# Windowed attention blocks of a hybrid encoder: negated maximum, sink exponential and row scaling moved from VectorE to ScalarE

## The chip, the cores and the metric

The kernel runs on one core of one Trainium2 chip. A core has five engines that run their own queues in order: PE (TensorE, matrix products and transposes; PEld are its weight loads), DVE (VectorE), ACT (ScalarE), POOL (GpSimd) and SP (SyncE, which here only issues DMAs). They wait for one another through semaphores. The metric is the device time of one execution in microseconds (us), the median of three runs.

## The reference, cut to what matters

The program is a two-layer encoder over 512 tokens and 1024 channels. In each layer three token mixers read one projection: windowed attention (6 query heads, 2 key/value heads), a gated DeltaNet in chunks of 64 tokens, and an RWKV-7 scan; then come an output projection and a gated MLP. The change lies in the softmax of the attention:

```python
m = jnp.maximum(jnp.max(s, -1, keepdims=True), sk)      # sk: the head's sink logit
p = jnp.exp(s - m)
p = p / (jnp.sum(p, -1, keepdims=True) + jnp.exp(sk - m))
o = jnp.einsum('bnhgqk,bnkhd->bnqhgd', p.astype(v.dtype), vw)
```

A block of 128 queries sees its own 128 keys and those of the neighbouring blocks: 384 keys in the two middle blocks, 256 in the two outer ones.

## The kernel before, in words

Everything is float32. Long products (`product`, lines 332 to 334) are done as three passes over split operands, for which ACT and POOL prepare the weights (L321, L322).

`attn_head` does one pair of query heads (g = 0, 1) as a generator of four blocks. There are three such pairs, so 12 blocks per layer and 24 in the program. A block goes through these steps, with their lines before the change:

- L886, PE: two score products into PSUM.
- L887, DVE: adds the mask, writes the scores to SBUF (`cv`) and gives the row maximum with the sink in it (`mx`); a second small instruction reads the maximum out.
- L891, DVE: sink minus maximum (`es`). L892, DVE: negated maximum (`nmx`). L893, ACT: exponential of `es`. All are 128x2.
- L896, ACT, once for each g: exponential of the scores with `nmx` as bias; a small instruction then reads the row sums (`den`).
- L897 and L898, DVE: `den` plus `es`, and its reciprocal.
- L900, DVE, once for each g: the rows of `cv` times the reciprocal.
- L903, PE: two or three 128x128 transposes. L905, ACT: their copy out of PSUM. L907, PE: the products with the values. At the end of a head pair L909 copies the result.

The blocks have no stage of their own. In `layer` they are interleaved with the DeltaNet:

```python
for i in range(31):
    next(both_ways)
    if i % 6 == 5:
        next(att, None)
```

`both_ways` is `invert_both`: a forward substitution on 32x32 blocks, 30 steps, each of one multiply (L432) and one add (L433) on DVE, in which every instruction needs the one before it. So five attention blocks are issued in the inversion. Four stream transposes on DVE (L440, L441) end it, and `finish_inverse` follows: small PE products (L455, L461) with ACT copies (L457, L465, L469) between them. Then comes `dn_scan`: 8 steps, each a chain of PE products (L806, L817, L794) and DVE instructions (L813, L822, L796, L802), with output products (L832, L833) beside it; in each of its steps one more block is issued until the 12 are done. Long products of the gate projection (L974 to L977 read them) and of the output projection fill PE in between. The order on each engine is not the order of the text: a scheduler places each instruction by its own costs when the program is built, so that a change of one instruction's engine moves others too.

Of the kernel before, what the change touches and what calls it, by code (L numbers as in the profile page):

```python
# [10 lines left out]
AF = mybir.ActivationFunctionType  # L11
# [104 lines left out]
def trunk(tc, t, out):  # L116
    nc = tc.nc
    V, S, G, PE = nc.vector, nc.scalar, nc.gpsimd, nc.tensor
    mult, add, sub, mx, mn = ALU.mult, ALU.add, ALU.subtract, ALU.max, ALU.min
# [15 lines left out]
    def ps(stream, shape=(P, T)):  # L135
        return psp.tile(list(shape), F32, tag="ps" + stream, bufs=PS_BUFS[stream], name=nm("ps"))
# [4 lines left out]
    def t2(stream, *free, dt=F32):  # L141
        return bp.tile([P, *(free or (T,))], dt, tag="t" + stream, bufs=T_BUFS[stream], name=nm("t" + stream))

    def cv(*free, dt=F32):
        return bp.tile([P, *(free or (T,))], dt, tag="cv", bufs=8, name=nm("cv"))
# [13 lines left out]
    def tiny(*free, tag="tiny"):  # L159
        if len(free) > 1:  # L160
            lo = W + DEPTH * NPAR + 2 * T + 48 * small_at.setdefault(tag, len(small_at))
            names = " ".join("abc"[: len(free)])
            return fixed[:, lo : lo + math.prod(free)].rearrange(f"p ({names}) -> p {names}", **dict(zip("abc", free)))
        return bp.tile([P, *free], F32, tag=tag, bufs=1 if len(free) > 1 else 3, name=nm(tag))


    W = _CONST.shape[1]
# [6 lines left out]
    def C(name):  # L174
        a, n = CONSTS[name]
        return cst[:, a : a + n]
# [697 lines left out]
    def attn_head(l, tq, q, k, vt, dst):  # L874
        po = ps("r")
        for nb in range(4):
            k0, k1 = max(0, nb - 1), min(3, nb + 1)
            nk = k1 - k0 + 1
            W = P * nk
            m0 = P * (k0 - nb + 1)  # L880
            scs = [cv(), cv()]
            mxt = tiny(2, tag="mx")
            for g in range(2):
                hs = slice(64 * g, 64 * g + 64)
                pss = ps("r")
                PE.matmul(pss[:, :W], q[hs, P * nb : P * nb + P], k[hs, P * k0 : P * k0 + W], start=True, stop=True)  # L886
                V.tensor_tensor_reduce(scs[g][:, :W], pss[:, :W], C("attm")[:, m0 : m0 + W], 1.0, sinkb[l][:, tq + 3 * g : tq + 3 * g + 1], add, mx, mxt[:, g : g + 1])  # L887
            sk = sinkb[l][:, tq : 6 : 3]
            nmx = tiny(2, tag="nmx")
            es = tiny(2, tag="es")  # L890
            V.tensor_tensor(es, sk, mxt, sub)  # L891
            V.tensor_scalar(nmx, mxt, -1.0, None, mult)  # L892
            S.activation(es, es, AF.Exp)  # L893
            den = tiny(2, tag="den")
            for g in range(2):
                S.activation(scs[g][:, :W], scs[g][:, :W], AF.Exp, bias=nmx[:, g : g + 1], accum_out=den[:, g : g + 1])  # L896
            V.tensor_tensor(den, den, es, add)  # L897
            V.reciprocal(den, den)  # L898
            for g in range(2):
                V.tensor_scalar(scs[g][:, :W], scs[g][:, :W], den[:, g : g + 1], None, mult)  # L900
                pp = ps("r")
                for j in range(nk):
                    PE.transpose(pp[:, P * j : P * j + P], scs[g][:, P * j : P * j + P], ident)  # L903
                pt = t2("r")
                S.activation(pt[:, :W], pp[:, :W], AF.Copy)  # L905
                for j in range(nk):
                    PE.matmul(po[64 * g : 64 * g + 64, P * nb : P * nb + P], vt[:, k0 + j, 64 * g : 64 * g + 64], pt[:, P * j : P * j + P], start=j == 0, stop=j == nk - 1)  # L907
            yield
        S.activation(dst, po, AF.Copy)  # L909


    def layer(l, norm, xd, last):
# [81 lines left out]
        def attention():  # L994
            for tq in range(3):
                yield from attn_head(l, tq, qs[tq], k, vt, yt[tq])
# [155 lines left out]
```

## Time and profile before

| | |
|---|---|
| runs | 1709.49, 1710.0, 1717.93 us, median 1710.0 |
| the profiled execution | 1722.8 us, of which the span 1721.0 us |
| busy share of the span | PE 90%, weight loads 70%, DVE 57%, ACT 46%, POOL 37% |
| mean granted TensorE clock | 0.931 of full speed |

The trace is of the profiled execution, so its stretches add up to the span of 1721.0 us and not to the median. The share of an engine is an average over stages with different limits. The stretch from 315 to about 450 us is the inversion, its finish and the DeltaNet scan of layer 0, and the same stretch of layer 1 begins at about 1158 us. In these the attention blocks lie.

### The profile page before, as it was taken

The numbers are of one execution on the slowest core, as the hardware profiler recorded it, in microseconds if no ns is written. First come the engines' busy times: TensorE is split into PE (matmuls) and PEld (weight loads), VectorE is DVE, ScalarE is ACT, GpSimd is POOL, SyncE is SP. The second block draws the span as 40 slices with busy tenths as digits, with TensorE's granted clock in tenths as the row PEclk, the third lists the DMA queues.
The fourth block names the chain that finished last, engine by engine and source line by source line (L and its number), as shares of the span: only waits on it lengthen the run. The fifth ranks groups of instructions, "written<-read, shape, count | busy, mean of one in ns | idle before, by whom it ended". The sixth has DMA issues, their size and how long they took to land. (4 is left out here: it accounts for less than half of the span.)

```text
span 1721.0 us, 29049 instructions
## 1 busy us (share of the span) xinstructions
PE 1544.2 (90%) x11500; PEld 1208.7 (70%) x11500; DVE 973.5 (57%) x1595; ACT 792.0 (46%) x1493; POOL 638.7 (37%) x510
## 2 busy tenths in 40 slices
PE   7988889569999999999998887983899999999997
PEld 4676666347778888888876666652677788888885
DVE  6578946875535557731136797579563555555001
ACT  5547453355444444433336654351734544444321
POOL 4321323101265554445552112420104555555553
PEclk9989979669999999999999998995799999999998
DMA  6221211100143333333442012220003333333331
GB/s 185 73 57 38 56 38 44 37 2 20 36 122 96 98 98 95 96 104 114 119 101 68 25 45 50 55 70 1 4 19 93 102 95 97 98 99 114 101 101 65
DMA packets 230536, 126.07 MB, mean 73 GB/s; under 512 B 23656, under 2 KB 221416, under 8 KB 230400
## 3 DMA queue, kind: packets, MB, share of 16 engines
q1 hardware_dynamic: 228624, 121.02, 25.0%
q10 hardware_dynamic: 1776, 3.20, 0.6%
q8 instruction: 90, 1.47, 0.3%
q14 instruction: 46, 0.38, 0.1%
HBM read 117.84 MB, written 6.34 MB: 72 GB/s over the span
## 5 line engine op out<-in xcount | busy, mean ns | idle before, releaser
L322 POOL TENSOR_TENSOR wl<-wr,wh 128x512 fp32r<-128x512 f32 (+1 forms) x408 | 553.6, 1363 | 753.2 <-ACT wh L321 664.2
L332 PE MATMUL ps<-hh,wh 128*128 128x512 f32 x1248 | 505.2, 405 | 22.1 <-ACT wh L321 19.6
L333 PE MATMUL ps<-hl,wh 128*128 128x512 f32 x1248 | 504.5, 404 | 0.0
L334 PE MATMUL ps<-hh,wl 128*128 128x512 f32 x1248 | 500.9, 401 | 0.4 <-POOL wl L322 0.4
L321 ACT ACTIVATE wh<-wr 128x512 fp32r<-128x512 f32 (+1 forms) x408 | 246.2, 615 | 330.8 <-PE ps L333 262.4
L332 PEld LDWEIGHTS ps<-hh,wh 128*128 128x128 f32 x1248 | 237.8, 191 | 80.9 <-ACT wh L321 20.4
L333 PEld LDWEIGHTS ps<-hl,wh 128*128 128x128 f32 x1248 | 238.0, 191 | 56.8 <-issue 4.2
L334 PEld LDWEIGHTS ps<-hh,wl 128*128 128x128 f32 x1248 | 237.5, 190 | 56.8 <-issue 3.9
L1104 DVE TENSOR_TENSOR p<-ps,p 128x512 f32<-128x512 f32 x16 | 11.1, 692 | 196.6 <-PE ps L334 196.6
L332 PE MATMUL ps<-p,wh 128*128 128x512 f32 x256 | 99.6, 389 | 0.0
L333 PE MATMUL ps<-p,wh 128*128 128x512 f32 x256 | 99.6, 389 | 0.0
L334 PE MATMUL ps<-p,wl 128*128 128x512 f32 x256 | 99.6, 389 | 0.0
L903 PE MATMUL ps<-fixed,cv 128*128 128x128 f32 x120 | 24.9, 340 | 62.4 <-DVE cv L900 62.0
L1081 DVE TENSOR_TENSOR tr<-ps,rb 128x512 f32<-128x512 f32 x44 | 30.4, 691 | 80.9 <-PE ps L334 80.8
L292 POOL TENSOR_TENSOR tr<-tr,tr 128x512 f32<-128x512 f32 x32 | 42.6, 1332 | 70.4 <-ACT tr L285 59.9
L903 PEld LDWEIGHTS ps<-fixed,cv 128*128 128x128 f32 x120 | 16.0, 168 | 72.5 <-issue 44.8
L1084 DVE SCALAR_TENSOR_TENSOR td<-tr,fixed,td 128x511 f32<-128x511 f32 x44 | 42.8, 972 | 37.7 <-ACT td L1083 37.7
L285 ACT ACTIVATE tr<-p 128x512 f32<-128x512 f32 x36 | 22.6, 628 | 85.9 <-DVE p L1104 64.4
L791 POOL TENSOR_TENSOR sm<-sm,fixed 128x384 f32<-128x384 f32 x12 | 10.8, 896 | 121.5 <-DVE sm L820 64.5
L333 PEld LDWEIGHTS ps<-p,wh 128*128 128x128 f32 x256 | 48.1, 188 | 10.1
L332 PEld LDWEIGHTS ps<-p,wh 128*128 128x128 f32 x256 | 48.1, 188 | 10.1
L1084 DVE SCALAR_TENSOR_TENSOR tr<-td,fixed,tr 128x511 f32<-128x511 f32 x44 | 33.9, 771 | 37.5 <-ACT tr L1083 37.5
(294 smaller groups left out, 2559.7 us busy)
## 6 DMA issues: line engine op xcount, KB each, us to landing
wr<-ffn_w_up SPq DMA_DIRECT2D x176, 256.0 KB, 2.8
wr<-w_in SPq DMA_DIRECT2D x88, 256.0 KB, 2.9
wr<-ffn_w_down SPq DMA_DIRECT2D x80, 256.0 KB, 2.9
wr<-w_in SPq DMA_DIRECT2D x24, 128.0 KB, 2.4
p<-scr ACTq DMA_DIRECT2D x12, 256.0 KB, 3.5
wr<-w_out SPq DMA_DIRECT2D x32, 96.0 KB, 2.6
wr<-w_out SPq DMA_DIRECT2D x16, 192.0 KB, 2.9
p<-xt SPq DMA_DIRECT2D x8, 256.0 KB, 5.0
```

The costliest lines, as they stand in the source:

```text
L285: S.activation(sq, xk, AF.Square)
L292: G.tensor_tensor(acc, self.acc, sq, add)
L321: S.activation(hi[:, :n, :], raw[:, :n, :], AF.Copy)
L322: G.tensor_tensor(lo[:, :n, :], raw[:, :n, :], hi[:, :n, :].bitcast(F32), sub)
L332: PE.matmul(o, wh, xh, start=k == 0, stop=False)
L333: PE.matmul(o, wh, xl, start=False, stop=False)
L334: PE.matmul(o, wl, xh, start=False, stop=k == n - 1)
L791: G.tensor_tensor(gs, state, flat(gl, step), mult)
L903: PE.transpose(pp[:, P * j : P * j + P], scs[g][:, P * j : P * j + P], ident)
L1081: V.tensor_tensor(u, o, nf.rb, mult)
L1084: V.scalar_tensor_tensor(a[:, 1:], u[:, :-1], w(0), a[:, 1:], mult, add)
L1104: V.tensor_tensor(x1[j], o, x1[j], add)
```

## The change

Three pieces of a block go from DVE to ACT. The negated maximum becomes an ACT copy with scale -1. The subtraction for the sink and its exponential over both heads become one ACT exponential for each head, with the negated maximum as bias, each placed behind that head's score exponential. The scaling of the rows by the reciprocal becomes an ACT copy with a column as scale.

```diff
             nmx = tiny(2, tag="nmx")
             es = tiny(2, tag="es")
-            V.tensor_tensor(es, sk, mxt, sub)
-            V.tensor_scalar(nmx, mxt, -1.0, None, mult)
-            S.activation(es, es, AF.Exp)
+            S.activation(nmx, mxt, AF.Copy, scale=-1.0)
             den = tiny(2, tag="den")
             for g in range(2):
                 S.activation(scs[g][:, :W], scs[g][:, :W], AF.Exp, bias=nmx[:, g : g + 1], accum_out=den[:, g : g + 1])
+                S.activation(es[:, g : g + 1], sk[:, g : g + 1], AF.Exp, bias=nmx[:, g : g + 1])
             V.tensor_tensor(den, den, es, add)
             V.reciprocal(den, den)
             for g in range(2):
-                V.tensor_scalar(scs[g][:, :W], scs[g][:, :W], den[:, g : g + 1], None, mult)
+                S.activation(scs[g][:, :W], scs[g][:, :W], AF.Copy, scale=den[:, g : g + 1])
```

In the changed kernel the lines of a block are L891 (negated maximum), L894 (score exponential), L895 (sink exponential), L896 and L897 (sum and reciprocal), L899 (scaling), L902 (transposes), L904 (their copy), L906 (products with the values) and L908.

The scheduler moves other instructions with it. On DVE, in the inversion of layer 0 at the second block (`cv_2948` and `cv_2949` are its scores, `pair_sq` the matrix under inversion), the difference reads:

```order
 L432 TENSOR_TENSOR cv_2887<-pair_sq 128x396
+L433 TENSOR_TENSOR pair_sq<-pair_sq,cv_2887 128x2x22x9
 L887 ISA cv_2948,mx_2950<-ps_2951,fixed 128x384
 L887 ISA mx_2950 128x1
-L433 TENSOR_TENSOR pair_sq<-pair_sq,cv_2887 128x2x22x9
+L432 TENSOR_TENSOR cv_2887<-pair_sq 128x420
 L887 ISA cv_2949,mx_2950<-ps_2954,fixed 128x384
 L887 ISA mx_2950 128x1
-L432 TENSOR_TENSOR cv_2887<-pair_sq 128x420
-L891 TENSOR_TENSOR es_2958<-fixed,mx_2950 128x2
-L892 TENSOR_SCALAR nmx_2957<-mx_2950 128x2
 L433 TENSOR_TENSOR pair_sq<-pair_sq,cv_2887 128x2x21x10
```

One more inversion instruction now stands ahead of each of the block's two maxima.

On ACT, in the finish of the inversion of layer 0 with the fifth block in it (`cv_3099` and `cv_3100`; `p_1880` and `p_2690` are matrices into which the inverse is written):

```order
+L469 ACTIVATE p_1880<-p_3137 32x8x32
+L894 ACTIVATE cv_3099,den_3111<-cv_3099,nmx_3108 128x256
+L895 ACTIVATE es_3109<-fixed,nmx_3108 128x1
+L894 ACTIVATE cv_3100,den_3111<-cv_3100,nmx_3108 128x256
+L895 ACTIVATE es_3109<-fixed,nmx_3108 128x1
+L469 ACTIVATE p_2690<-p_3137 32x8x32
 L457 ACTIVATE td_3146<-ps_3145 32x512 x2
+L469 ACTIVATE p_2690<-p_3137 32x8x32 x2
+L899 ACTIVATE cv_3099<-cv_3099,den_3111 128x256
+L899 ACTIVATE cv_3100<-cv_3100,den_3111 128x256
 L469 ACTIVATE p_2690<-p_3137 32x8x32
+L904 ACTIVATE tr_3122<-ps_3119 128x256
```

The two scalings now stand in ACT's queue among the copies of the inverse.

On PE, in a step of the scan of layer 0 with a wide block, it stood before in this order (`ps_4031` and `ps_4041` take the transposes, `ps_4114` is the scan's new state, `tr_4035` and `tr_4045` the copied transposes):

```order
L903 MATMUL ps_4031<-fixed,cv_4011 128x128 x3
L903 MATMUL ps_4041<-fixed,cv_4012 128x128 x3
L833 MATMUL ps_4070<-p_2780,sm_3992 64x64
L832 MATMUL ps_4070<-p_2767,sm_3893 64x64
L833 MATMUL ps_4070<-p_2780,sm_3992 64x64
L817 MATMUL ps_4114<-sm_4111,p_1921 64x64
L907 MATMUL ps_3896<-tr_4035,at_2291 64x128 x3
L907 MATMUL ps_3896<-tr_4045,at_2291 64x128 x3
L817 MATMUL ps_4114<-sm_4111,p_1921 64x64 x3
L817 MATMUL ps_4114<-sm_4111,p_2731 64x64 x4
L817 MATMUL ps_4114<-sm_4111,p_2820 64x64 x4
```

and with the change in this one:

```order
L833 MATMUL ps_4070<-p_2780,sm_3992 64x64
L333 MATMUL ps_4436<-hl_4402,wh_4441 128x512
L817 MATMUL ps_4114<-sm_4111,p_1921 64x64
L902 MATMUL ps_4031<-fixed,cv_4011 128x128 x3
L817 MATMUL ps_4114<-sm_4111,p_1921 64x64 x2
L902 MATMUL ps_4041<-fixed,cv_4012 128x128 x3
L817 MATMUL ps_4114<-sm_4111,p_1921 64x64
L817 MATMUL ps_4114<-sm_4111,p_2731 64x64 x4
L817 MATMUL ps_4114<-sm_4111,p_2820 64x64
L906 MATMUL ps_3896<-tr_4035,at_2291 64x128 x3
L906 MATMUL ps_3896<-tr_4045,at_2291 64x128 x3
L817 MATMUL ps_4114<-sm_4111,p_2820 64x64 x3
```

The transposes now stand among the state products instead of ahead of them, and a product of the output projection (`ps_4436`) has come between.

## Rows read from the trace of the kernel before

**Rows 1.** The page: busy time and share, and the chain that ended last.

```profile
PE 1544.2 (90%) x11500; PEld 1208.7 (70%) x11500; DVE 973.5 (57%) x1595; ACT 792.0 (46%) x1493; POOL 638.7 (37%) x510
PE 31%; DVE 6%; issue 2%; ACT 1%; POOL 1%; DMA 0%; POOLq 0%; DVEq 0%; SPq 0%; ACTq 0%
```

**Rows 2.** Busy time by stretches: engines (instructions), granted clock (PEclk), DMA.

```profile
315.00:364.00 49.00, 19.15 (x74) 11.74 (x76) 45.36 (x114) 10.01 (x33) 0.21 (x1) 0.57 0.02 6
364.00:376.00 12.00, 7.24 (x169) 5.93 (x170) 10.14 (x16) 9.12 (x24) 0.00 (x0) 0.50 0.00 1
376.00:383.00 7.00, 6.12 (x138) 4.02 (x138) 1.40 (x6) 6.52 (x16) 0.00 (x0) 0.95 0.01 4
383.00:393.00 10.00, 10.00 (x150) 7.38 (x145) 0.56 (x1) 7.58 (x19) 0.00 (x0) 0.53 0.01 2
400.00:450.00 50.00, 46.95 (x860) 37.57 (x859) 32.15 (x107) 22.64 (x66) 7.15 (x7) 1.00 0.07 18
1350.00:1700.00 350.00, 350.00 (x1539) 289.64 (x1539) 140.72 (x183) 145.53 (x231) 183.12 (x139) 1.00 0.33 95
```

**Rows 3.** Single lines: duration in ns min/median/max, first and last start, shapes.

```profile
L900 DVE TENSOR_SCALAR cv<-cv,den x48: 332/394/420, 328.1 to 1290.2; 128x256 f32<-128x256 f32 x24, 128x384 f32<-128x384 f32 x24
L896 ACT ACTIVATE cv<-cv,nmx x48: 491/548/604, 326.0 to 1288.9; 128x256 f32<-128x256 f32 x24, 128x384 f32<-128x384 f32 x24
L893 ACT ACTIVATE es<-es x24: 189/203/205, 325.9 to 1288.3; 128x2 f32<-128x2 f32 x24
L475 ACT ACTIVATE p<-tr,fixed x16: 723/724/725, 29.3 to 910.2; 128x512 f32<-128x512 f32 x16
```

**Rows 4.** DVE in time, inversion, layer 0: start, us, instruction, idle and its releaser.

```profile
336.23 0.59 DVE L432 TENSOR_TENSOR cv<-pair_sq 128x420 f32<-128x420 f32 x1
336.88 0.59 DVE L433 TENSOR_TENSOR pair_sq<-pair_sq,cv 128x420 f32<-128x420 f32 x1
339.47 0.63 DVE L433 TENSOR_TENSOR pair_sq<-pair_sq,cv 128x456 f32<-128x456 f32 x1
340.68 0.64 DVE L432 TENSOR_TENSOR cv<-pair_sq 128x468 f32<-128x468 f32 x1
341.35 0.65 DVE L433 TENSOR_TENSOR pair_sq<-pair_sq,cv 128x468 f32<-128x468 f32 x1
...
360.41 0.43 DVE L433 TENSOR_TENSOR pair_sq<-pair_sq,cv 128x260 f32<-128x260 f32 x1
361.28 0.38 DVE L432 TENSOR_TENSOR cv<-pair_sq 128x216 f32<-128x216 f32 x1
```

**Rows 5.** DVE in time, the row maxima of the second and third block.

```profile
333.06 0.62 DVE L887 CUSTOM_DVE_ANT_0 cv<-ps,fixed 128x384 f32<-128x384 f32 x1 [0.29 <-PE ps L886]
335.69 0.62 DVE L887 CUSTOM_DVE_ANT_0 cv<-ps,fixed 128x384 f32<-128x384 f32 x1 [1.51 <-PE ps L886]
...
345.83 0.62 DVE L887 CUSTOM_DVE_ANT_0 cv<-ps,fixed 128x384 f32<-128x384 f32 x1 [0.37 <-PE ps L886]
```

**Rows 6.** ACT in time, end of the finish of the inversion, layer 0.

```profile
388.67 0.78 ACT L465 ACTIVATE p<-ps 32x256 f32<-32x256 f32 x2 [1.44 <-PE ps L461]
```

**Rows 7.** PE in time, one step of the scan with a wide block.

```profile
436.09 0.92 PE L794 MATMUL ps<-sm,cv 64*64 64x64 f32 x24
438.43 0.91 PE L806 MATMUL ps<-sm,p 64*64 64x64 f32 x24 [0.53 <-DVE sm L802]
439.91 0.94 PE L903 MATMUL ps<-fixed,cv 128*128 128x128 f32 x6
443.91 0.92 PE L794 MATMUL ps<-sm,cv 64*64 64x64 f32 x24
```

**Rows 8.** DVE in time, the same step.

```profile
437.35 0.16 DVE L891 TENSOR_TENSOR es<-fixed,mx 128x2 f32<-128x2 f32 x1
437.50 0.55 DVE L796 TENSOR_TENSOR sm<-ps,fixed 128x384 f32<-128x384 f32 x1
439.44 0.75 DVE L900 TENSOR_SCALAR cv<-cv,den 128x384 f32<-128x384 f32 x2
```

## The prediction

> **What bounds the kernel now.** I read the page first, by engine and by chain. PE is busy for 90% of the span and has 31% of the chain that ended last; DVE has 6% of that chain, ACT 1% [rows 1]. So work taken from DVE counts only where DVE holds PE up, and I looked for such stretches in the view by stretches [rows 2]. The reader is to see four kinds in layer 0. From 315 to 364 DVE is busy 45.36 of 49 us and PE 19.15, at a mean clock of 0.57: the inversion, bound by its chain on DVE. From 364 to 393 DVE fades, and ACT is busy 9.12 of 12, 6.52 of 7 and 7.58 of 10 us: the finish of the inversion, in which ACT and PE take turns. From 400 to 450, the scan, PE is busy 46.95 of 50 at the full clock, and 3.05 us of idle is all that could be won there. In the long products from 1350 to 1700 PE has no idle at all, and no attention block. Layer 1 repeats the pattern. After that I read the groups of the lines concerned, then DVE, ACT and PE in time through these stretches.
>
> **The inversion: what DVE loses.** Five of a layer's twelve blocks are issued there, and for four of them the scalings stand between two instructions of the inversion's chain. An add that is followed at once by the next multiply holds DVE for its duration and 0.03: 340.68 to 341.35 is 0.67 for 0.64. With the pair of 384-wide scalings between, 339.47 to 340.68 is 1.21 where 0.66 would do, so the pair costs 0.55. With the 256-wide pair, 360.41 to 361.28 is 0.87 against 0.46: 0.41 [rows 4]. Two middle blocks and two outer ones would give 2 x 0.55 + 2 x 0.41 = 1.9 us a layer. In the first block the two scalings are split up and cost about half, so I take 1.8. The small L891 and L892 lie between a multiply and the add that waits for it: 336.23 to 336.88 is 0.65 for an instruction of 0.59, where 0.62 would do without them [rows 4]. They hide in that wait, and their going gives 0.03 a block, which I cost at nothing.
>
> What is late next is the maximum of the following block. L887 already waited 1.51 and 0.37 us for the scores from PE [rows 5]. Those scores stand in PE's queue behind the transposes of the block before, and these will not come earlier: the reciprocal is now taken one inversion instruction later, since it waits for two more exponentials on ACT, and the scaling on ACT is 0.50 to 0.61 long where DVE took 0.33 to 0.42 [rows 3]. For the second block I find the scores about 0.3 us later. The scheduler has put one more inversion instruction (0.6 us) ahead of L887, which fills part of the wait. Carried through: DVE is ahead by 0.35 us after the second block's maxima, by 0.6 after the third's, by 0.65 after the fourth's, and the fourth's own scalings add 0.4. So the transposes that end the inversion start 1.05 us earlier. The bounds are 0 (all given back at L887) and 1.8 us and the waits of 1.51 and 0.37, together 3.7, a layer.
>
> **The finish of the inversion: what ACT gains in work.** The fifth block falls here. ACT gets one small copy and two small exponentials in place of one, each about 0.11 us in a row of overlapping instructions (0.20 alone), and two scalings of 0.50 less 0.09 of overlap: 1.1 us. The size of a scaling is interpolated: a column bias with 256 and 384 elements takes 0.49 and 0.60, a column scale with 512 takes 0.72, and these lie on one line [rows 3]. DVE's reciprocal for them comes behind the third transpose, about when ACT is done with the two L457 ahead of the scalings; they hold up the L469 and L465 queued behind them, on which PE's L806 waits. Against that ACT has slack of 1.44 us before its last L465 [rows 6]. In the new order I find the last L806 up to 0.4 us later than before, but by then PE has done six more long products, which at 350 / 1539 = 0.227 us each [rows 2] are 1.4 us. So the 1.05 of the inversion survives this stage nearly whole: I take +0.05, with bounds of 0 and +1.1 a layer.
>
> **The scan: seven blocks, one a step.** One step of the chain, from L794 to L794, is 436.09 to 443.91, 7.82 us [rows 7]. DVE no longer has L891 and L892 ahead of L796, so this begins at least 0.15 us earlier (437.35 to 437.50) [rows 8], which shortens PE's 0.53 us wait before L806 [rows 7]. On the other side the scalings, which began on DVE at 439.44 [rows 8] and let PE transpose at 439.91 [rows 7], come later: 0.2 for the added exponentials, 0.1 for the hop to ACT, 0.13 for the longer scaling. PE's first transpose is about 0.43 later, and the second, behind another 0.5 us on ACT, later still. But the new order lets most of the state products L817 run before the value products that need these transposes. Replayed with the rows' durations the step comes to 7.86 us, with one more long product (0.23) inside it: 0.2 us to the good. Over seven steps that is 1.4; as not all steps have a long product to fill the hole, I take 0.5 a layer. The bounds: 1.4 gained, and 7 x 0.43 = 3.0 lost if each delay counts whole.
>
> **The sum.** A layer: -1.05 + 0.05 - 0.5 = -1.5 us; both layers: -3.0. Against the profiled execution's own 1722.8 that is 1719.8. That execution is 12.8 us above the median of the runs, 1710.0, so I carry the difference over: 1707.0 us.
>
> **The rivals.**
>
> *The clock recovers sooner.* The granted clock is 0.50 to 0.57 through the inversion, 0.95 from 376 to 383, and 0.53 again from 383 to 393 though PE is busy all ten [rows 2]: two levels, 1.2 and 2.4 GHz. The new order has more long products in that second stretch, in runs of four. The Trainium skill ("TensorE: Matmul & The Clock Gate", "What's actually happening") says that throttled is the default and that activity releases it; the first stretch agrees with it, with PE at 19.15 of 49 us busy and 0.57, and the ten busy us at 0.53 do not. If the full clock held from 383 on, ACT's 7.58 us would be the floor of those ten, 2.4 us won a layer, and up to 4.7 where ACT's share shrinks with it: some 3.5 x 2 on top of the 3.0, so 1700. For it: the denser products; against: new waits of PE for ACT in the same stretch.
>
> *The scalings are on the path in every block.* Slower. A wide pair takes 0.51 + 0.60 = 1.11 us on ACT (the first less 0.09 of overlap) and 0.75 on DVE [rows 3, 8], so it ends 0.36 later; if PE waits ahead of the transposes with nothing else to run, 24 x 0.36 = 8.6 us: 1718.6. It decides as soon as PE stands idle before L902 in most blocks; in the scan PE has products to put there, in the inversion its clock is halved and its queue holds nothing else. The Trainium skill ("ScalarE: Activation LUTs", "Rules for kernel authors") says to use VectorE and not ScalarE for a multiply; rows agree in the direction, 0.41 against 0.60 for the wide rows, and this rival is what the rule would make of the whole.
>
> *The clock is lost.* From 376 to 383 PE did 6.12 us of work at 0.95 [rows 2]; with the transposes waiting for ACT just before, it might stay at the low level, the 6.12 become 12.2, and 5.2 a layer are lost: 1710 + 10.4 - 2 x 0.5 = 1719.4.
>
> *Nothing is left.* L887 waits for PE in each block, DVE's 1.8 us turn into those waits, and the scan comes out even: 1710.
>
> **How the numbers follow.** A difference under 0.5%, 8.5 us, is what a measurement of this kernel cannot tell from no change. Chances: forecast 0.58, nothing left 0.15, clock sooner 0.12, scalings on the path 0.09, clock lost 0.06. The forecast's own range is 1702 to 1712: its bounds a layer are wide, but the stages share PE, and the runs shown are 8.4 apart. The range 1699 to 1718 takes in the clock rival's middle and leaves out the last two cases' upper halves. Faster by over 0.5% needs under 1701.5: most of the clock rival, and 0.03 of the forecast, 0.12 in all. Slower needs over 1718.5: half of the path rival, two thirds of the lost clock and some spread, 0.10. Between lies 0.78.
>
> **What would show it.** In the changed profile: the four transposes of the inversion begin 0.7 to 1.4 us earlier after its first multiply; L887's idle in the second and third block is 0.3 to 0.7 us each at the least; L899 takes 0.50 and 0.61; ACT is busier by about 24 x 1.4 us, DVE less busy by about 24 x 1.1; a step of the scan stays at 7.7 to 8.0 us; the clock from 376 to 393 shows the same two levels. I am wrong if the inversion ends as late as before, if the steps of the scan move by more than 0.3 us, or if the stretch at half clock before the scan changes by more than 3 us.

## The result and the profile after

The change makes the kernel slower. Five runs of the changed kernel took 1723.56 to 1728.62 us, median 1727.76, and five of the kernel before, beside them, 1709.49 to 1717.93, median 1710.57: a ratio of 1.0084, 95% interval 1.0059 to 1.0109. Here and below a ratio is taken over all the runs, not from the two medians. The forecast was 1707.0, its range ended at 1718. A second set gave medians of 1730.02 against 1715.43, a ratio of 1.0079 (1.0052 to 1.0105).

The page of the changed kernel, by engine and by chain (answers to [rows 1]):

```profile
PE 1549.4 (90%) x11500; PEld 1205.1 (70%) x11500; DVE 937.4 (54%) x1499; ACT 829.8 (48%) x1589; POOL 641.9 (37%) x510
PE 32%; DVE 6%; ACT 1%; issue 1%; POOL 1%; DMA 0%; POOLq 0%; DVEq 0%; SPq 0%; ACTq 0%
```

The work went where the prediction said: DVE 36.1 us less, ACT 37.8 us more, where it had expected about 24 x 1.1 = 26.4 and 24 x 1.4 = 33.6. The engine shares do not say where the time was lost; the stages do. Here are the inversion, its finish and the scan in the view by stretches, cut at the starts of the first L427, L440 and L813 and of the last L796 on DVE. The columns are the stretch, its length, busy time and instructions of PE, weight loads, DVE, ACT and POOL, then the granted clock, the DMA share and GB/s. First the kernel before, layer 0 and the finish of layer 1:

```profile
320.51:364.06 43.55, 19.21 (x74) 11.80 (x76) 39.85 (x104) 8.82 (x29) 0.21 (x1) 0.58 0.00 1
364.06:391.69 27.63, 21.99 (x441) 16.22 (x441) 11.54 (x22) 22.45 (x55) 0.00 (x0) 0.62 0.01 2
391.69:444.93 53.24, 50.40 (x891) 39.59 (x893) 34.66 (x110) 25.00 (x70) 8.37 (x8) 0.98 0.06 17
1206.99:1234.65 27.66, 22.04 (x441) 16.19 (x441) 11.55 (x23) 22.50 (x55) 0.00 (x0) 0.62 0.01 2
```

then the changed kernel, layer 0 and layer 1:

```profile
315.31:357.98 42.67, 19.18 (x72) 11.60 (x72) 37.78 (x87) 14.65 (x44) 0.22 (x1) 0.54 0.00 1
357.98:393.69 35.71, 31.30 (x448) 21.14 (x447) 10.71 (x16) 23.88 (x59) 0.00 (x0) 0.50 0.01 2
393.69:449.83 56.14, 51.80 (x886) 39.53 (x888) 28.88 (x86) 33.79 (x94) 7.83 (x8) 0.98 0.06 16
1165.74:1208.34 42.60, 19.19 (x72) 11.59 (x72) 37.79 (x87) 14.65 (x44) 0.22 (x1) 0.58 0.00 0
1208.34:1239.84 31.50, 26.63 (x448) 17.93 (x448) 10.73 (x17) 22.75 (x58) 0.00 (x0) 0.62 0.01 2
1239.84:1294.00 54.16, 50.59 (x886) 38.82 (x888) 28.90 (x86) 34.84 (x98) 7.83 (x8) 1.00 0.06 17
```

The inversion is 0.9 us shorter (43.55 to 42.67). The finish is 8.1 us longer in layer 0 (27.63 to 35.71) and 3.8 in layer 1, where the kernel before took 27.66. The scan is 2.9 us longer in layer 0 and 0.6 in layer 1 (53.57 before). In layer 0 the finish went wholly at the low level of the clock, 0.50 where it was 0.62. In layer 1 the mean clock is 0.62 in both kernels, and the finish is longer all the same; both layers of a second profile of the changed kernel (e14 below) are like this one, with 31.6 and 31.5 us at 0.62. So 3.8 to 3.9 us is the usual loss; the 8.1 us, with the clock at the low level throughout, stand in one layer of four.

The six stages of the two layers add up to 13.5 us more, but the two profiled executions differ by 5.5 (spans of 1726.5 and 1721.0). The changed kernel's was 5.2 us ahead when its first inversion began, at 315.31 against 320.51, and it gained 2.5 more between the layers, where no attention block lies. That differs from one execution to the next: in e14 the first inversion of the changed kernel begins at 319.59. Between the two later profiles, e14 and e4 (the kernel before), the six stages differ by 11.9 us and the spans by 15.0.

What PE did there. The kernel before, PE in time: start, duration, instruction, tiles, count:

```profile
373.71 0.88 PE L455 MATMUL ps<-p,p 32*32 32x32 f32 x26
374.52 0.80 PE L332 MATMUL ps<-hh,wh 128*128 128x512 f32 x1
375.12 0.63 PE L903 MATMUL ps<-fixed,cv 128*128 128x128 f32 x2
375.39 0.78 PE L333 MATMUL ps<-hl,wh 128*128 128x512 f32 x1
375.97 0.63 PE L334 MATMUL ps<-hh,wl 128*128 128x512 f32 x1
376.39 0.53 PE L332 MATMUL ps<-hh,wh 128*128 128x512 f32 x1
376.86 0.65 PE L907 MATMUL ps<-tr,at 128*64 128x128 f32 x4
...
380.24 0.92 PE L886 MATMUL ps<-at,at 64*128 64x384 f32 x4
```

The fifth block's transposes (L903) come behind the second group of L455, with four long products (L332 to L334) around them. The clock rises at 376.7, and the sixth block's two score products (L886) later run side by side at the full clock, both in 0.92 us. The changed kernel at the same place:

```profile
367.35 0.69 PE L902 MATMUL ps<-fixed,cv 128*128 128x128 f32 x2
...
369.20 0.80 PE L332 MATMUL ps<-hh,wh 128*128 128x512 f32 x1
369.93 1.12 PE L906 MATMUL ps<-tr,at 128*64 128x128 f32 x4
370.98 0.69 PE L902 MATMUL ps<-fixed,cv 128*128 128x128 f32 x2
371.60 1.65 PE L886 MATMUL ps<-at,at 64*128 64x384 f32 x2
373.17 1.11 PE L906 MATMUL ps<-tr,at 128*64 128x128 f32 x4
374.22 1.65 PE L886 MATMUL ps<-at,at 64*128 64x384 f32 x2
375.79 1.06 PE L461 MATMUL ps<-p,td 32*32 32x32 f32 x32
376.67 1.90 PE L455 MATMUL ps<-p,p 32*32 32x32 f32 x64
378.49 0.80 PE L333 MATMUL ps<-hl,wh 128*128 128x512 f32 x1
```

The first transposes (L902) now come before the second group of L455, one long product follows, and three of the others stand behind a row of small pieces. The sixth block's two score products are parted by four value products of the fifth (L906; the expectations below call them addition products) and take 1.65 us each. PE itself does not rest from there on, yet the granted clock is that of the low level for the whole of the next row, again by stretches:

```profile
366.00:396.00 30.00, 30.00 (x388) 20.05 (x390) 3.25 (x9) 20.10 (x49) 0.00 (x0) 0.50 0.01 2
```

The Trainium skill ("TensorE: Matmul & The Clock Gate", "What's actually happening") says that the low level is the default and that activity releases it. PE's 30.00 busy us in 30 at 0.50 do not bear that out as the profile counts busy time; what else the chip goes by, no run here shows.

ACT is not what holds the end of the finish up. Its last L465 still waits for PE as before, 1.42 us against 1.44 [rows 6]:

```profile
388.90 0.76 ACT L465 ACTIVATE p<-ps 32x256 f32<-32x256 f32 x2 [1.42 <-PE ps L461]
```

### The profile page after: what moved, and what is told of

Read it like the earlier page. It is cut to its first block, busy times and chain, and to the rows that moved or that the text cites. A ratio compares the mean times of both kernels' runs of the same rounds, so it can differ in the third digit from the quotient of the medians.

```text
span 1726.5 us, 29078 instructions
## 1 busy us (share of the span) xinstructions
PE 1549.4 (90%) x11500; PEld 1205.1 (70%) x11500; DVE 937.4 (54%) x1499; ACT 829.8 (48%) x1589; POOL 641.9 (37%) x510
## 5 line engine op out<-in xcount | busy, mean ns | idle before, releaser
L332 PE MATMUL ps<-hh,wh 128*128 128x512 f32 x1248 | 502.2, 403 | 23.4 <-ACT wh L321 20.9
L334 PE MATMUL ps<-hh,wl 128*128 128x512 f32 x1248 | 500.0, 401 | 0.4 <-POOL wl L322 0.4
L332 PEld LDWEIGHTS ps<-hh,wh 128*128 128x128 f32 x1248 | 236.4, 190 | 83.5 <-ACT wh L321 21.8
L334 PEld LDWEIGHTS ps<-hh,wl 128*128 128x128 f32 x1248 | 236.4, 189 | 55.2 <-issue 3.7
L1103 DVE TENSOR_TENSOR p<-ps,p 128x512 f32<-128x512 f32 x16 | 11.1, 692 | 198.3 <-PE ps L334 198.3
L332 PE MATMUL ps<-p,wh 128*128 128x512 f32 x256 | 99.6, 389 | 0.0
L334 PE MATMUL ps<-p,wl 128*128 128x512 f32 x256 | 99.6, 389 | 0.0
L902 PE MATMUL ps<-fixed,cv 128*128 128x128 f32 x120 | 27.8, 350 | 62.4 <-ACT cv L899 62.2
L902 PEld LDWEIGHTS ps<-fixed,cv 128*128 128x128 f32 x120 | 15.6, 168 | 73.5 <-ACT cv L899 70.2
L292 POOL TENSOR_TENSOR tr<-tr,tr 128x512 f32<-128x512 f32 x32 | 42.9, 1342 | 55.2 <-ACT tr L285 44.2
L1083 DVE SCALAR_TENSOR_TENSOR td<-tr,fixed,td 128x511 f32<-128x511 f32 x44 | 39.1, 888 | 34.8 <-ACT td L1082 34.8
L332 PEld LDWEIGHTS ps<-p,wh 128*128 128x128 f32 x256 | 48.0, 188 | 10.1
L334 PEld LDWEIGHTS ps<-p,wl 128*128 128x128 f32 x256 | 48.0, 188 | 9.9
```

Source lines behind the costliest of these rows:

```text
L292: G.tensor_tensor(acc, self.acc, sq, add)
L332: PE.matmul(o, wh, xh, start=k == 0, stop=False)
L334: PE.matmul(o, wl, xh, start=False, stop=k == n - 1)
L1083: V.scalar_tensor_tensor(a[:, 1:], u[:, :-1], w(0), a[:, 1:], mult, add)
```

## The experiments

Theory A: the loss is made in the finish by the new order on PE, and by the clock that follows from it. Theory B: the scalings on ACT come late in each of the 24 blocks, and PE waits for them. The table gathers the runs. The stages are differences of DVE's starts as above, layer 0 / layer 1, in us. "Full clock" says when, behind L440, the granted clock stood at its upper level, rounded to 1 us; a last number without an end stands for the rise after which it stayed there to the end of the scan. The ratio is against the kernel before in the same set. Stages and clock are those of one execution: of e7 and e11 it was the fastest of their runs, of e3 and e6 the slowest, of e2 one within 2 us of the slowest.

| kernel | ratio (95%) | inversion | finish | scan | full clock |
|---|---|---|---|---|---|
| before | | 43.6 / 43.6 | 27.6 / 27.7 | 53.2 / 53.6 | 13 to 19, 30 / 13 to 20, 30 |
| e4 before again | | 43.7 / 43.5 | 25.0 / 27.6 | 52.3 / 53.5 | 13 / 13 to 19, 30 |
| changed | 1.0084 (1.0059-1.0109) | 42.7 / 42.6 | 35.7 / 31.5 | 56.1 / 54.2 | 38 / 24 |
| e14 changed again | 1.0079 (1.0052-1.0105) | 42.6 / 42.6 | 31.6 / 31.5 | 55.0 / 54.2 | 24 / 24 |
| e1 small work only | 1.0058 (1.0037-1.0078) | 43.5 / 43.2 | 34.3 / 34.4 | 53.7 / 53.6 | 37 / 37 |
| e2 scalings only | 1.0048 (1.0016-1.0079) | 42.7 / 42.6 | 29.7 / 29.7 | 60.1 / 59.6 | 13 to 20, 34 to 48, 54 / 14 to 20, 34 to 48, 54 |
| e3 not the fifth block | 1.0011 (0.9987-1.0035) | 42.6 / 42.6 | 27.7 / 27.6 | 56.2 / 55.4 | 14 to 20, 31 / 14 to 21, 31 |
| e5 first four blocks | 0.9974 (0.9949-1.0000) | 42.7 / 42.5 | 27.6 / 27.7 | 53.8 / 53.6 | 14 to 21, 31 / 14 to 20, 31 |
| e6 fifth block only | 1.0102 (1.0065-1.0139) | 43.6 / 43.7 | 33.3 / 35.7 | 54.2 / 56.4 | 30 to 40, 43 / 41 to 44, 47 |
| e7 before, PE kept busy | 1.0010 (0.9985-1.0034) | 46.7 / 45.2 | 26.4 / 22.9 | 51.9 / 52.2 | to 6, 24 / to 6, 13 |
| e8 changed, PE kept busy | 1.0082 (1.0050-1.0115) | 44.3 / 42.9 | 29.8 / 29.8 | 56.9 / 56.4 | to 2, 32 / to 2, 32 |
| e9 changed, order held | 1.0019 (0.9998-1.0040) | 42.5 / 41.6 | 28.1 / 28.0 | 55.0 / 54.2 | 14 to 20, 24 / 13 to 19, 23 |
| e10 e9, scan held too | 1.0008 (0.9989-1.0027) | 42.6 / 42.6 | 31.1 / 27.6 | 55.9 / 53.8 | 14 to 21, 35 / 14 |
| e11 first four, PE kept busy | 1.0022 (1.0002-1.0043) | 44.1 / 44.0 | 25.6 / 26.9 | 53.1 / 54.1 | to 6, 16 / to 5, 9 to 19, 29 |
| e12 before, order of changed | 1.0109 (1.0080-1.0138) | 43.3 / 43.6 | 35.2 / 37.5 | 54.5 / 54.9 | 31 / 37 |
| e13 before, pair parted | 0.9981 (0.9961-1.0002) | 43.5 / 42.7 | 26.9 / 31.7 | 50.8 / 50.8 | 13 / 26 |
| e15 e5 with e13 | 0.9952 (0.9934-0.9969) | 42.6 / 41.6 | 27.3 / 27.1 | 50.7 / 50.8 | 14 / 13 |

**Parts of the change (e1, e2).** e1 keeps the scaling on DVE:

```diff
-                S.activation(scs[g][:, :W], scs[g][:, :W], AF.Copy, scale=den[:, g : g + 1])
+                V.tensor_scalar(scs[g][:, :W], scs[g][:, :W], den[:, g : g + 1], None, mult)
```

> Only the small work is on ACT (inversion of the maximum, the sink's exponentials); all 24 scalings of the rows stay on DVE. Theory A (the loss is the clock: in the new order PE is not given its 7 us at the high level in the finish of the inversion, and is held at the low level until the scan begins): the order of PE in the finish has the last two score products of 384 columns apart, with an addition product between them, as in the changed kernel, so most of the loss is there, +8 to +14 us against the kernel before, with the time from L440 to the first L813 at 31 to 36 us a layer. Theory B (the scalings on ACT are late in each of the 24 blocks, 0.36 us or more each, and PE waits for them): no loss, -2 to +1 us, and 27.6 us from L440 to L813.

e2 is the kernel before with this line edited the other way.

> Only the 24 scalings of the rows are on ACT; the inversion of the maximum and the sink's exponential are as before. Theory A (clock in the finish of the inversion): the order of PE there is that of the kernel before up to the transposes of the fifth block, then the two score products stand apart; between before and after, +3 to +14 us, and the loss shows between L440 and L813 and goes with the time at the low level there. Theory B (late scalings in each block): the whole loss, +14 to +17 us, spread over the blocks of the scan as well, 0.5 to 0.7 us for each step.

e1 moves no scaling and still has a finish of 34.3 us: Theory B cannot make that loss. e2 keeps the long products at the fifth block's transposes, and its finish is only 2 us longer. Its scan was a miss for both theories: 60 us, because the clock fell again from 48 to 54 us after L440. That need not be so in each of its executions: its runs go from 1714.9 to 1737.3 us, and the profiled one took 1735.8. The two parts' losses do not add up to the whole; each has its own order on PE and its own clock.

**By block (e3, e5, e6).** A condition on the block's number chooses between the lines before and after:

```diff
+            new = 4 * tq + nb != 4
```

with `< 4` in e5 and `== 4` in e6.

> As the changed kernel, but the fifth block of each layer (the one whose transposes fall in the finish of the inversion) is as before; 22 of 24 blocks changed. Theory A (clock in the finish): the order of PE in the finish is that of the kernel before but for one long product, so its high level comes back and the loss shrinks to 0 to +5 us. Theory B (late scalings): 11/12 of the loss stays, +13 to +16 us.

> Only the first four blocks of each layer (those whose transposes fall in the inversion) are changed; the other eight are as before. The order of PE in the finish and in the scan is that of the kernel before. Theory A (the loss is the clock, set by where the fifth block's transposes stand): L427 to L440 42.6 us (0.9 shorter), L440 to L813 25 to 27.7 us with the high level from 12 to 19 us after L440, the scan 52.3 to 53.6 us; in all -2 us against the kernel before, which the comparison cannot tell from none. Theory B (each changed block costs its share): 4/12 of the loss, +3 to +5 us, and a finish or a scan longer than before.

> Only the fifth block of each layer is changed, 2 of 24. Theory A: the order of PE in the finish is that of the changed kernel, so the high level of 7 us is lost, L440 to L813 is 31 to 36 us as there, and most of the loss comes with this one block: +6 to +14 us. Theory B: 1/12 of the loss, about +1 us, and 27.6 us from L440 to L813.

One block in twelve brings the whole loss, and with 17.9 us by the medians more than the 6 to 14 expected; the eleven others (e3) cost nothing that can be told. e6, its finish in layer 1 by stretches:

```profile
1211.42:1247.07 35.65, 30.95 (x447) 20.88 (x447) 10.94 (x18) 23.74 (x59) 0.00 (x0) 0.50 0.01 1
```

e5 keeps the gain of the inversion, as the prediction priced it, and loses nothing behind it.

**The kernel before again (e4).**

> The kernel before, unchanged, for a second profile: the profile that the prediction rests on was of an execution 12 us above the median of its runs. If the low-clock stretches of the finish belong to the order of the work, L440 to L813 is again 27.6 us in both layers with the high level for 7 us; if they are a matter of the single execution, it will differ by several us. Where the other 12 us were lost shows as a stretch that is shorter now.

Both, in one execution: layer 1 repeats 27.6 us, in layer 0 the second fall of the clock is absent and the finish takes 25.0. So one source of the spread of the kernel before, 1709.5 to 1727.5 us over all sets, is its own clock. Of the 7.2 us between the spans of its two profiles, 3.6 lie in the finish and the scan of layer 0 and 2.6 between the layers.

**The order alone (e9, e12, e13).** These edges queue one PE instruction behind another on PE without a wait. e9 is the changed kernel with:

```diff
+        behind(first_transpose[l, block 5], last_L455[group 2])
...
+                    behind(score_product[l, block 6, g], last_L455[group 3])
```

> The changed kernel whole, all 24 blocks, with three order edges a layer on PE (no wait, only issue order): the fifth block's first transpose behind the second group of L455, the sixth block's score products behind the third, which is where they stand in the kernel before. Theory A (the loss of the finish is the order on PE and the clock that follows from it): the high level from 12 to 19 us after L440 comes back, L440 to L813 is 27 to 29 us, and the whole falls from +17 to +1 to +6 us against the kernel before, what stays being the scan (2.5 us a layer) less the inversion (0.9). If the scalings on ACT made the finish late by their own work: 31 us or more from L440 to L813, and +10 us or more.

e12 is the kernel before with edges for the opposite:

```diff
+        behind(first_L455[group 2], first_transpose[l, block 5])
...
+                behind(first_value_product[l, block 5, g=1], score_product[l, block 6, g=0])
+                behind(first_L455[group 3], score_product[l, block 6, g=1])
+                behind(second_long_product, score_product[l, block 6, g=1])
```

> The kernel before, nothing moved between engines, with order edges on PE alone (no wait) that make the fifth block stand in the finish as in the changed kernel: its transposes before the second group of L455, the sixth block's two score products apart with addition products between, and the long products from the second on behind them. Theory A (the order on PE, and the clock that follows, is the whole loss of the finish): the high level from 12 to 19 us after L440 is lost, L440 to L813 is 31 to 36 us, the whole +6 to +14 us. If the scalings on ACT are needed for the loss: 27 to 29 us and +0 to +3 us.

e13 is the kernel before with only the second and third of these.

> The kernel before with the sixth block's two score products (64 rows each, run side by side when adjacent) set apart in the finish, an addition product between them; the long products stay among the fifth block's transposes as before. If the parted pair is what takes the clock: L440 to L813 31 us or more. If the long products at the transposes are what raises it: the high level comes as before or up to 2 us later, L440 to L813 is 28 to 30 us, the parted pair costing 1.2 to 2 us by itself (1.65 us for one at the low level, 0.92 for the pair at the high one), the whole +2 to +5 us.

e9 and e12 together show that the order on PE makes the loss. The finish of e9, every scaling on ACT:

```profile
363.27:391.37 28.10, 22.84 (x448) 16.54 (x448) 10.61 (x17) 22.72 (x58) 0.00 (x0) 0.70 0.01 2
```

and of e12, nothing moved off DVE:

```profile
353.14:388.33 35.19, 30.48 (x455) 20.97 (x456) 12.51 (x25) 23.65 (x60) 1.36 (x2) 0.56 0.01 2
```

All 24 scalings on ACT with these pieces in their old places: 28.1 and 28.0 us. None on ACT with the pieces in their new places: 35.2 and 37.5, and a loss of 1.0109, again above the 6 to 14 us expected. e12's order is not the changed kernel's in full: 24 and 23 long products stand in its finish, 19 in that of the changed kernel and 13 before. So it shows that an order on PE can make a loss of this size with nothing moved, not that every part of that order has its share in the changed kernel's.

e13 was to show which part matters, and leaves it open. The whole is not slower, where +2 to +5 us were expected, but its scan is 2.5 and 2.8 us shorter than before, and its two layers differ in the finish:

```profile
363.66:390.53 26.87, 21.28 (x448) 15.30 (x449) 11.61 (x22) 23.13 (x57) 0.00 (x0) 0.76 0.01 2
1200.55:1232.26 31.71, 26.76 (x448) 18.43 (x449) 11.54 (x23) 23.19 (x57) 0.00 (x0) 0.60 0.01 2
```

In both the order is the same, and the full clock came 13 us after L440 in one and 26 in the other, where the finish is as long as the changed kernel's. e2 has the pair parted too and got the full clock at 13 and 14 us. So parting the pair does not by itself keep the full clock away. The order sets what is likely, not what is certain; the changed kernel's 38 and 24 say the same.

**PE kept busy (e7, e8, e11).** Products that nothing reads, where PE idles:

```diff
+            keep_warm({0: 60, 1: 18, 2: 22, 3: 18, 4: 14}.get(4 * tq + nb, 0))
```

> The kernel before with useless long products behind the score products of the first five blocks (60, 18, 22, 18 and 14 of 512 columns, 0.23 us each at the high level), where PE is idle in the inversion; nothing reads them. Theory A: PE keeps the high level through the inversion and the finish; L440 to L813 falls from 27.6 to 21 to 25 us, the waits of L887 for the scores in the inversion shrink by 1 to 2 us, and the whole is 6 to 14 us below the kernel before. If the granted clock does not follow PE's activity, or if ACT bounds the finish: 27 us as before, or more by what the useless products delay.

> The changed kernel with the same useless products. Theory A: its finish loses the whole excess over that of the kernel before with the same products (the two differ there by 2 us at most, against 4 to 8 without them), and the two whole times differ by what the scan costs, 1 to 3 us a layer less 0.9 from the inversion, so 0 to +5 us. If ACT's longer work made the finish late, and not the clock: 4 to 8 us a layer stay between the two.

> The change in the first four blocks of a layer alone, and useless long products of 512 columns on PE where it idles at the low level: 9 behind the fourth block's score products, 14 behind the fifth's, and 3 behind each of the four groups of L455 in the finish; nothing reads them. Theory A (the finish goes at the speed of PE's clock): the high level stands at the start of the finish or soon after, L440 to L813 is 21 to 25 us against 27.6, and the whole is 4 to 12 us below the kernel before. If the small products of the finish let the clock fall all the same, or ACT bounds it: 27 us or more, and no gain.

As remedies they failed, e7 and e11 against a forecast gain of 4 us or more: the products delayed the inversion by up to 3 us, and the clock fell soon after L440 all the same, in a stretch of 32x32 products with waits between them. The expected match of e7 and e8 failed too. But from the first L455 on PE has the same order of instructions in their finishes, and the clock differs. Layer 1 of e7 and of e8:

```profile
1200.64:1223.56 22.92, 20.12 (x441) 14.49 (x440) 9.86 (x13) 19.40 (x47) 0.00 (x0) 0.85 0.01 2
```

```profile
1209.81:1239.62 29.81, 28.80 (x443) 20.65 (x443) 9.62 (x11) 20.44 (x48) 0.00 (x0) 0.53 0.01 2
```

With the mean clock at 0.85 it takes 22.92 us, at 0.53 29.81. Of the 6.9 us, 6.1 lie behind the first L455, which starts 3.8 and 4.6 us after L440; ahead of it e8 has four more value products. Within e7 alone the two layers, same order throughout, take 26.4 us at 0.68 and 22.9 at 0.85.

**The scan (e10).** e9, and each block's first transpose behind the last L817 of the step:

```diff
+            if 1 <= i < 7:
+                behind(first_transpose[l, block 5 + i], last_L817)
```

> As the run with the three edges, and in the scan the first transpose of each block is queued behind the last L817 of the step, so that a block's transposes stand together and the three groups of L817 too. Theory A' (the scan is longer since PE's runs of concurrent 64x64 products are cut up by single groups of transposes): L817 takes 6.6 us a scan on PE in place of 8.3 to 9.0, the scan 53 to 54.5 us in place of 54.2 to 56.9, and the whole is -3 to +3 us against the kernel before. Theory B' (the scan is longer since PE waits for the scalings on ACT): the transposes and all behind them come later still, the scan is 56 us or more.

L817 and the transposes are whole again (in this file L820 is L817, L911 is L902, L797 is L794 and L916 is L906):

```profile
1239.64 0.91 PE L820 MATMUL ps<-sm,p 64*64 64x64 f32 x24
1240.49 0.87 PE L911 MATMUL ps<-fixed,cv 128*128 128x128 f32 x6
1241.58 0.28 PE L797 MATMUL ps<-sm,cv 64*64 64x64 f32 x2
1241.78 1.14 PE L916 MATMUL ps<-tr,at 128*64 128x128 f32 x12
```

L817 takes 6.5 and 5.8 us of PE, added up to the next instruction's start, where e9 has 8.3 in both. But the scan is no shorter beyond what executions differ by (55.9 / 53.8 us against e9's 55.0 / 54.2, layer 0 with the full clock only from 35 us): L794 is now cut up instead (its first two products stand ahead of the last row) and takes 0.5 us more, the score products L886 0.6, the output products L832 and L833 1.1. Theory A' holds for where the time was, and not for how to get it back; Theory B' does not hold, since transposes that come later still did not lengthen the scan of layer 1.

**The changed kernel again (e14), and a version that beats both (e15).**

> The changed kernel, unchanged, beside more runs of the kernel before: those of the kernel before spread from 1710 to 1727 us, and five of them stood beside the changed kernel so far. Theory A: +8 to +17 us, L440 to L813 31 to 36 us in both layers. If the five were lucky runs and the change costs only what the scan shows: +2 to +5 us.

e14 confirms the size. Both its layers have the full clock from 24 us.

> Both gains together: the change in the first four blocks of a layer alone (0.9 us a layer in the inversion), and the order edges that set the sixth block's score products apart (its scan took 50.8 us in place of 53.5). If the two add up: L427 to L440 42.6 us, the scan 50.8 us, L440 to L813 27 to 32 us depending on when the high level comes, and the whole 5 to 9 us below the kernel before. If they do not, since the order moves the phase of the finish: no gain that the comparison can tell.

They add up: 0.9974 x 0.9981 is 0.9955, and e15 has 0.9952. e15, layer 0 by stretches:

```profile
320.89:363.47 42.58, 19.10 (x72) 11.59 (x72) 37.78 (x87) 14.65 (x44) 0.21 (x1) 0.58 0.00 1
363.47:390.78 27.31, 22.06 (x449) 15.87 (x449) 11.60 (x23) 23.31 (x57) 0.00 (x0) 0.75 0.01 2
390.78:441.52 50.74, 47.84 (x886) 38.02 (x888) 34.77 (x111) 24.27 (x70) 8.72 (x8) 1.00 0.07 18
```

42.6 us of inversion, 27.3 of finish at 0.75, 50.7 of scan at 1.00: 1711.81 us beside 1719.42, 0.48% faster over all runs. The scan is shorter in e13 and e15 though nothing in it was moved between engines: 20 long products are done in the finish already, where 13 were, and 12 in the scan, where 17 were, and PE waits 0.8 us for L802 there in place of 2.2. The edges were not put in for that; it is their side effect, and no run takes it apart.

## Why the prediction was wrong, step by step

- **The inversion, -1.05 a layer: right.** -0.9 and -1.0 measured, and the same within 0.1 us in e2, e3, e5, e10 and e14, in which the first four blocks' scalings are on ACT too and nothing else delays the inversion. In layer 1 of e9, e13 and e15 the order edges take about 1 us more off it, most of that from L887's waits. The mechanism is the one forecast. In layer 0 DVE is busy 2.1 us less (the prediction's 1.8 is 1.7 by its own terms, 2 x 0.55 + 0.41 + about 0.2), and L887 gives back 0.84: its waits for the scores grow from 2.32 to 3.16, most of that at the fourth block. The rows for the second, third and fourth block, to be held against [rows 5]:

```profile
328.18 0.62 DVE L887 CUSTOM_DVE_ANT_0 cv<-ps,fixed 128x384 f32<-128x384 f32 x1 [0.32 <-PE ps L886]
330.79 0.62 DVE L887 CUSTOM_DVE_ANT_0 cv<-ps,fixed 128x384 f32<-128x384 f32 x1 [1.48 <-PE ps L886]
340.68 0.62 DVE L887 CUSTOM_DVE_ANT_0 cv<-ps,fixed 128x384 f32<-128x384 f32 x1 [0.60 <-PE ps L886]
351.37 0.48 DVE L887 CUSTOM_DVE_ANT_0 cv<-ps,fixed 128x256 f32<-128x256 f32 x1 [0.76 <-PE ps L886]
```

- **The finish, +0.05 a layer: the step that failed.** It measured +8.1 and +3.8, in e14 +3.9 and +3.8. The prediction saw the new order and read from it that six more long products were done by the last L806, at 0.227 us each: "So the 1.05 of the inversion survives this stage nearly whole". Two things were wrong. The 0.227 is a price at the full clock; the long products ran at the low level, 0.43 us apart (starts at 379.08, 379.51 and 379.94). And it asked how late ACT's copies would be, not what the earlier transposes do to PE: the sum has no term for the clock. The transposes were taken from among the long products, and the 7 us at the full clock that had followed [rows 2] did not come in layer 0; in the other three layers it came about 11 us later, when the attention pieces had been done at the low level. In layer 0 PE is busy 9.3 us longer (31.30 against 21.99); added up by line, 3.4 are the six more long products, 2.4 the parted pair (2 x 1.65 - 0.92), most of the rest the same work at half the clock. In layer 1, with the mean clock as before, PE is busy 4.6 us longer (26.63 against 22.04): 2.8 are score products, 1.5 transposes and value products, 0.9 the six long products, and L806, now at the full clock, takes 0.6 less.

- **The scan, -0.5 a layer: wrong in sign, inside its bounds.** It measured +2.9 and +0.6, in e14 +1.8 and +0.6. The 0.6 flatters the change, as the scans of the kernel before began with about 2 us at the low level: at the full clock throughout, the kernel before took 52.3 (e4, layer 0) and the changed one 54.2 to 55.0. With only the small work on ACT (e1) it is 53.7 and 53.6, so the scalings make it. In layer 0 half of the 2.9 is busy time of PE (51.80 against 50.40) and half idle, of which only 0.4 are longer waits of transposes for a scaling and 1.2 longer waits of L806 for DVE's L802, less 0.1 elsewhere. The busy half is in runs of 64x64 products that are cut up. Before, a step's transposes stand together, as L903 in [rows 7], and L817 runs in one piece:

```profile
399.29 0.87 PE L903 MATMUL ps<-fixed,cv 128*128 128x128 f32 x6
...
402.77 0.92 PE L817 MATMUL ps<-sm,p 64*64 64x64 f32 x24
```

In the changed kernel the same step's transposes come one by one, and cut L817 in pieces:

```profile
402.49 0.79 PE L817 MATMUL ps<-sm,p 64*64 64x64 f32 x18
403.21 0.55 PE L902 MATMUL ps<-fixed,cv 128*128 128x128 f32 x3
403.69 0.33 PE L817 MATMUL ps<-sm,p 64*64 64x64 f32 x4
403.95 0.55 PE L902 MATMUL ps<-fixed,cv 128*128 128x128 f32 x3
404.43 0.27 PE L817 MATMUL ps<-sm,p 64*64 64x64 f32 x1
```

  L817's 168 products in the scan of layer 0, by stretches with that line alone, before and after:

```profile
391.69:444.93 53.24, 7.80 (x168) 0.98 0.06 17
```

```profile
393.69:449.83 56.14, 10.24 (x168) 0.98 0.06 16
```

  7.80 us becomes 10.24. The prediction's replay used the durations of the kernel before, in which the run is whole.

- **The rivals.** "The clock is lost" is the one that came nearest, at 1719.4 and a chance of 0.06. Its size per layer (5.2) lies between the two measured; its condition, that the transposes wait for ACT, was wrong: they come earlier (9.4 us after L440 for 11.1), and that is what breaks the order. "The scalings are on the path in every block" comes near the scan's size in layer 0 (7 x 0.36 = 2.5) by another mechanism, and falls for the rest with e1, e3 and e9. "The clock recovers sooner" was opposite. Of the signs written down, the last is the stretch at half clock before the scan: it grew from 23 to 38 us in layer 0, but only from 23 to 24 in layer 1 and in both layers of e14. It told in one layer of four; the length of the finish would have told in each.

With the order held the time would have been inside the range, though not by the forecast's sum: e9, with all of the change in it, is 1.0019 (0.9998 to 1.0040), where the forecast was 0.9982.

## What to carry to other kernels

Where a scheduler orders the work, moving a small operation to another engine moves other engines' order, and the cost can lie wholly there: compare PE's order in each stretch where its clock changes level, and price PE's instructions there at the low level. When a short stretch at the full clock sits in a stage bound by dependences, look at what runs on PE just before it and whether the change takes that away or puts it off. If only some of the moved instructions do harm, the change in the other blocks alone can keep the gain (e5), and an order edge can take the loss away (e9).

## What was not expected of the hardware

PE busy without a gap for 30 us at the low level; the same order of instructions with the rise at 13 us in one layer and 26 in the other (e13). What releases the clock there stays open.

Two 64-row score products side by side cost what one costs alone. The adjacent pair at the low level, kernel before:

```profile
344.15 1.65 PE L886 MATMUL ps<-at,at 64*128 64x384 f32 x4
```

1.65 us for both, and 1.65 for each when four value products stand between (371.60 and 374.22 in the changed kernel above). The Trainium skill ("TensorE: Matmul & The Clock Gate", "The mechanism") says that products on different parts of the array overlap; the rows agree, and add that the overlap is lost when products that take all 128 rows (L906, tiles 128*64) stand between the two.
